# Modulation products of a diffusion backbone run while the last queries of each mixer are rotated, with other rooms for their weights

## The chip, the cores and the metric

The kernel runs on one core of a Trainium2 chip. The metric is the device time of one execution in microseconds, and lower is better. TensorE does the matrix products and the transposes, VectorE (DVE in the rows), ScalarE (ACT) and GpSimd (POOL) the rest; SyncE (SP) issues most of the transfers. A framework lays out each engine's list of instructions before the kernel runs. On the chip every engine works through its own list in that order, and waits where an operand or a room isn't there yet.

## The reference

A backbone of two layers over 512 latent tokens and 256 context tokens, width 1024, in float32:

```python
# layer: SwiGLU (half step) -> token mixing -> SwiGLU (half step)
# each sub-layer:  u = rmsnorm(h, g_pre) * (1 + scale) + shift
#                  h = h + gate * rmsnorm(f(u), g_post)
# shift, scale, gate (9 vectors per layer) = silu(c) @ w_ada + b_ada
def _even_mixer(u, uc, ...):       # layer 0
    xa, ga, q, k, v = _split(u @ w_in, EVEN_SPLITS)
    ...                            # RG-LRU on xa; window attention on q, k, v
    q = _apply_rope(q...); k = _apply_rope(k...)
    o_b = _window_attention(q, k, v, kc, vc, sink_kg)      # 8 heads of 64, 2 kv heads
    y = jnp.concatenate([y_a, o_b], axis=-1) @ w_out
def _odd_mixer(u, uc, ...):        # layer 1
    q = _apply_rope(_rmsnorm(q, q_gain), rope)             # 8 heads of 128, 2 kv heads
    y = _dense_attention(q, k_all, v_all) @ w_out          # 512 queries, 768 keys
```

The modulation is a product of one vector (two: c and the context's) with a matrix of 1024 x 9216 for each layer.

## The kernel before

Tokens are in six tiles of 128 (t = 0 and 1 are the context, 2 to 5 the latents). A float32 product is made as three products of rounded high and low halves.

**Modulation in the background.** Each layer's 9 vectors are computed in blocks p of two vectors. `ada_steps(p)` is a generator: a step k loads two tiles of 128 x 1024 weights (`wa`, halves b = 0 and 1; one transfer of 512 KB each on SP's queue, L126), and does four products of 512 columns with the vector as stationary operand (L129), the four in columns 0-31, 32-63, 64-95 and 96-127 of the array, into one accumulator `ada`. A block has eight steps and a closing part (L136 to L167: bias, transposes, columns, gates). `tick(n)` runs the next n steps where it stands in the code, and the attention calls it three times in each of its groups (a group is a token tile and a kv head). Blocks 3 to 6 run in the even mixer, 7 and 8 in the odd one, and their tiles take rooms `whi` and `wlo`, four each, which the split weights of other phases use. `flush()` at the attention's end runs what is left.

**The mixers.** The q/k/v products of both mixers (`type2`) are done by token tile at their end: the last weights of tile t, then `qkv(t)` or `qf(t)`. There the queries are rotated on VectorE (rope: L1108 to L1111 even, L1393 to L1396 odd), split into halves (`qp`, L1119 and L1120, even), and transposed on TensorE into a PSUM room `ps` (`qT`, L1139, `kT`, L1144; odd `oqT`, L1437). `ps` has two rooms. In the even mixer, the scores of the first two groups (`s`) are made there for t = 4 and 5, and their maximum is one reduction (`sm<-s`, L1171). The attention then makes scores (`s`, L1298 to L1301; odd `os`), transposes the exponentials (`pT`, L1332; odd `opT`) and multiplies them with the values (`av`). Output products follow (`eo0a`; odd `oo0a`).

**Rooms.** `raw` are the three rooms into which weights come before they are split (L179 to L181); `G0` and `G1` hold the gates, one room each, loaded after the attention.

Of the kernel before, what the change touches and what calls it, by code (L numbers as in the profile page):

```python
# [12 lines left out]
F32 = mybir.dt.float32  # L13
# [4 lines left out]
P = 128  # L18
D = 1024
# [9 lines left out]
class Net:  # L29
# [83 lines left out]
    def ada_steps(self, p):  # L113
        nc, cp = self.nc, self.cp
        acc = self.adatile(f"ada{p}")
        for k in range(KD):
            raws = []
            for b in range(2):
                l, j = divmod(2 * p + b, 9)
                src, name = self.a["w_ada"][l, k * P:(k + 1) * P, j * D:(j + 1) * D], f"wa{p}_{k}{b}"  # L120
                if p > 2:

                    t = self.ws.tile([P, D], F32, tag=("whi", "wlo")[b], bufs=4, name=name)
                else:
                    t = self.ws.tile([P, D], F32, tag="bx", bufs=2, name=name)
                nc.sync.dma_start(t, src)  # L126
                raws += [t[:, 0:512], t[:, 512:]]
            for g in range(4):
                ins = nc.tensor.matmul(acc[32 * g:32 * g + 32, :], lhsT=self.sc[:, k, :],  # L129
                                       rhs=raws[g], start=(k == 0), stop=(k == KD - 1), skip_group_check=True)  # L130
                if p == 1:
                    self.late(ins)
            yield
        adt = self.bp.tile([P, 2, 512], F32, tag="bu", bufs=2, name=f"adt{p}")
        rows, post = adt[:, 0], adt[:, 1]
        nc.sync.dma_start(rows, self.a["b_ada"][p])  # L136
        nc.vector.tensor_add(rows, acc, rows)
        kinds = [(2 * p + b) % 9 % 3 for b in range(2)]
        if any(k != 2 for k in kinds):
            tp = self.adatile(f"adt{p}")  # L140
            for q in range(4):
                nc.tensor.transpose(tp[:, q * P:(q + 1) * P], rows[:, q * P:(q + 1) * P], self.ident)
            cols = cp.tile([P, 4, 2, 4], F32, name=f"cols{p}")
            nc.vector.tensor_copy(cols, tp.rearrange("p (q g w) -> p g w q", q=4, g=4)[:, :, 0:2, :])  # L144
            for b in range(2):
                i = 2 * p + b
                l, j = divmod(i, 9)
                if kinds[b] == 0:
                    self.modc[i] = (cols, 2 * b)
                elif kinds[b] == 1:  # L150
                    gs = cp.tile([P, 2, 2, 4], F32, name=f"gs{i}")
                    g = self.gpre[:, l * 3 + j // 3].rearrange("p (g q) -> p g q", g=2)
                    for v in range(2):
                        nc.vector.scalar_tensor_tensor(gs[:, :, v, :], cols[:, 2 * b:2 * b + 2, v, :], 1.0, g,
                                                       op0=ALU.add, op1=ALU.mult)
                    self.gscale[i] = gs
        for b in range(2):
            if kinds[b] != 2:
                continue
            i = 2 * p + b  # L160
            nc.sync.dma_start(post, self.a["post"][p])
            gp = post
            nc.vector.scalar_tensor_tensor(gp, rows, 1.0 if (i % 9) == 5 else 0.5, post, op0=ALU.mult, op1=ALU.mult)
            gd = self.dp.tile([2, D], F32, name=f"gd{i}")
            for h in range(2):
                q = 32 * (2 * b + h)
                nc.sync.dma_start(gd[:, h * 512:(h + 1) * 512], gp[q:q + 2, :])  # L167
            self.growd[i] = gd
# [812 lines left out]
    def even(self, u, gate_i, finish):  # L981
# [132 lines left out]
        def qkv(t, acc):  # L1114
            qk = roped(acc[:, 0:640], t, f"qk{t}")
            q, k = qk[:, 0:512], qk[:, 512:640]
            qp = sb.tile([P, 8, 2, 64], F32R, tag="bu", bufs=2, name=f"qp{t}")
            q3 = q.rearrange("p (h d) -> p h d", h=8)
            nc.scalar.activation(qp[:, :, 0, :], q3, AF.Copy)  # L1119
            nc.vector.tensor_sub(qp[:, :, 1, :], q3, qp[:, :, 0, :].bitcast(F32))  # L1120
            kp = sb.tile([P, 2, 2, 2, 64], F32R, tag="bu", bufs=2, name=f"kp{t}")
            k3 = k.rearrange("p (h d) -> p h d", h=2)
            for e in range(2):
                nc.scalar.activation(kp[:, 0, :, e, :], k3, AF.Copy)
            for e in range(2):
                nc.vector.tensor_sub(kp[:, 1, :, e, :], k3, kp[:, 0, :, e, :].bitcast(F32))
            if t % 3 == 0:
                qst["v"] = self.c3([P, 3, 2, 2, 64], F32R, f"vt{t}")
                qst["q"] = sb.tile([P, 3, 8, P], F32R, tag=("u0h", "u0l")[t // 3], name=f"qt{t}")
            vt = qst["v"][:, t % 3]  # L1130
            v3 = acc[:, 640:768].rearrange("p (h d) -> p h d", h=2)
            nc.scalar.activation(vt[:, :, 0, :], v3, AF.Copy)
            nc.vector.tensor_sub(vt[:, :, 1, :], v3, vt[:, :, 0, :].bitcast(F32))
            vs[t] = vt
            qt = qst["q"][:, t % 3]
            for h in range(2):
                tp = self.ps(f"qT{t}{h}").bitcast(F32R)
                for e in range(4):
                    nc.tensor.transpose(tp[:, e * P:(e + 1) * P], qp[:, 4 * h + e], self.identr)  # L1139
                nc.scalar.activation(qt[:, 4 * h:4 * h + 4, :], tp.bitcast(F32), AF.Copy)  # L1140
            qs[t] = qt
            tp = self.ps(f"kT{t}").bitcast(F32R)
            for e in range(4):
                nc.tensor.transpose(tp[:, e * P:(e + 1) * P], kp[:, e // 2, e % 2], self.identr)  # L1144
            for s in range(2):
                for h in range(2):
                    o = (2 * s + h) * P
                    nc.scalar.activation(kt[s][h][:, t * P:(t + 1) * P], tp[:, o:o + P].bitcast(F32), AF.Copy)
# [221 lines left out]
    def odd(self, u, gate_i, finish):  # L1370
# [17 lines left out]
        def roped(s3, t, nh, w, name):  # L1388
            o = sb.tile([P, nh, P], F32, tag="bx", bufs=2, name=name + "o")
            t2 = sb.tile([P, nh, P], F32, tag="by", bufs=3, name=name + "t")  # L1390
            bc = lambda x: x.unsqueeze(1).to_broadcast([P, nh, x.shape[-1]])
            tb = tab[t - 2][:, w]
            nc.vector.tensor_mul(o, s3, bc(tb[:, 0, :]))  # L1393
            nc.vector.tensor_mul(t2[:, :, 0::2], s3[:, :, 1::2], bc(tb[:, 1, 0::2]))
            nc.vector.tensor_mul(t2[:, :, 1::2], s3[:, :, 0::2], bc(tb[:, 1, 1::2]))
            nc.vector.tensor_add(o, o, t2)  # L1396
            return o
# [22 lines left out]
        def qf(t, acc):  # L1420
            s3 = acc.rearrange("p (h d) -> p h d", h=8)
            o = roped(s3, t, 8, 0, f"oq{t}")
            r = rms(s3, 8, f"oq{t}")
            rn = sb.tile([P, 2, 8], F32, name=f"orq{t}")
            for e in range(2):
                nc.vector.tensor_scalar(rn[:, e, :], r, (sc, -sc)[e], None, op0=ALU.mult)
            rq[t] = rn
            qt = []
            for s in range(2):
                i = 2 * (t - 2) + s  # L1430
                if i % 3 == 0:
                    qtt.append(sb.tile([P, 3, 8, P], F32R, tag=("u0h", "u0l", "u1h")[i // 3], name=f"oqt{i}"))
                qt.append(qtt[i // 3][:, i % 3])
            for h in range(2):
                tp = self.ps(f"oqT{t}{h}")
                for e in range(4):
                    nc.tensor.transpose(tp[:, e * P:(e + 1) * P], o[:, 4 * h + e, :], self.ident)  # L1437
                hs = slice(4 * h, 4 * h + 4)
                t3 = tp.rearrange("p (h n) -> p h n", h=4)
                nc.scalar.activation(qt[0][:, hs, :], t3, AF.Copy)  # L1440
                if t < 3:
                    nc.vector.tensor_sub(qt[1][:, hs, :], t3, qt[0][:, hs, :].bitcast(F32))
                    continue
                if h == 0:
                    whole = self.junk(f"oqr{t}").rearrange("p (h n) -> p h n", h=8)
                raw = whole[:, hs, :]
                nc.scalar.activation(raw, t3, AF.Copy)
                nc.gpsimd.tensor_sub(qt[1][:, hs, :], raw, qt[0][:, hs, :].bitcast(F32))
            qs[t] = qt
# [222 lines left out]
```

## Time and profile before

| | |
|---|---|
| three runs | 2595.28, 2600.66, 2603.51 us (median 2600.66) |
| profiled execution | 2593.1 us; span of its instructions 2591.3 |
| mean granted clock of TensorE | 0.988 |
| TensorE | 2489.6 us busy, 96% |
| VectorE | 1877.6 us, 72% |
| ScalarE | 1290.7 us, 50% |
| GpSimd | 373.3 us, 14% |

The shares are means over the whole span; what a change in a mixer is worth depends on the stretch in which it stands. The even mixer's attention lies at some 720 to 854 us, the odd one's at 2045 to 2160.

### The profile page before, as it was taken

To read this page: it belongs to the slowest core of one execution; us is meant where nothing else is said; L and a number is where in the kernel's file an instruction comes from. 1 tells how busy PE (TensorE), PEld (TensorE's weight loads), DVE (VectorE), ACT (ScalarE), POOL (GpSimd) and SP (SyncE) were. 2 spreads that over 40 slices of the span, in tenths; PEclk is the share of its full clock that TensorE was granted. 3 is DMA by queue.
4 is the path that set the end of the run, shared out by engine and by line. 5 is a ranking of instruction groups with operands and counts; after the bars stand their busy time and mean duration, and the time that the engine had idled before them with its cause. 6 is when DMAs were issued, how large, how long until landed. Compare 5 with 4: busy or idle time off the path is not lost.

```text
span 2591.3 us, 36846 instructions
## 1 busy us (share of the span) xinstructions
PE 2489.6 (96%) x13683; PEld 2188.9 (84%) x13683; DVE 1877.6 (72%) x2946; ACT 1290.7 (50%) x2346; POOL 373.3 (14%) x472
## 2 busy tenths in 40 slices
PE   7999999998999989999999899999998899999998
PEld 5999997878855779999887899998876667899986
DVE  5877777577677687878757787887586666888843
ACT  4433335556665564443456544444465556655532
POOL 4000000122022130000002300001122221300000
PEclk8999999999999999999999999999999999999999
DMA  7677767651387435555776355558764652544552
GB/s 279 215 244 242 242 222 268 227 188 51 111 297 266 166 106 184 199 180 193 270 245 228 136 187 181 194 193 280 238 233 145 209 180 74 191 130 136 158 174 92
DMA packets 187588, 502.37 MB, mean 194 GB/s; under 512 B 17944, under 2 KB 51912, under 8 KB 187408
## 3 DMA queue, kind: packets, MB, share of 16 engines
q1 hardware_dynamic: 157520, 392.27, 44.6%
q0 software_dynamic: 29888, 107.74, 11.7%
q8 instruction: 107, 1.75, 0.3%
q14 instruction: 73, 0.60, 0.1%
HBM read 397.33 MB, written 102.61 MB: 193 GB/s over the span
## 4 chain that ended last, share of the span: by engine, by line
PE 78%; DVE 7%; issue 7%; DMA 3%; ACT 3%; POOL 2%; SPq 0%; POOLq 0%; DVEq 0%; ACTq 0%
PE px L784 18%; PE py L784 12%; PE pz L784 12%; PE dy L729 8%; PE dx L729 5%; PE d11a L935 5%; PE ada L129 3%; PE oq1a L935 1%; PE gu L211 1%; PE gu L212 1%; PE eo0a L935 1%; PE gu L210 1%; PE qkv1a L935 1%; DMA dw<-in_w_down_dram 1%; PE pT L1332 1%
## 5 line engine op out<-in xcount | busy, mean ns | idle before, releaser
L831 ACT ACTIVATE cp<-px 128x384 f32<-128x384 f32 (+1 forms) x160 | 73.2, 457 | 207.3 <-PE px L784 207.2
L837 ACT ACTIVATE h<-cp 128x768 f32<-128x768 f32 (+1 forms) x80 | 63.3, 792 | 195.7 <-DVE cp L861 138.8
L623 POOL DMA_DIRECT2D wt<-wt x33 | 17.7, 537 | 706.6 <-DVE wt L622 681.4
L129 PE MATMUL ada<-wa,sc 128*32 128x512 f32 x512 | 83.4, 610 | 0.5 <-DVE cols L144 0.4
L831 ACT ACTIVATE cp<-pz 128x384 f32<-128x384 f32 (+1 forms) x80 | 37.0, 463 | 87.2 <-PE pz L784 87.0
L861 DVE TENSOR_TENSOR cp<-px,cp 128x768 f32<-128x768 f32 (+1 forms) x80 | 70.8, 884 | 5.1 <-PE px L784 5.0
L839 DVE TENSOR_TENSOR h<-cp,h 128x768 f32<-128x768 f32 (+1 forms) x80 | 71.2, 891 | 2.2
L670 DVE TENSOR_TENSOR dh_2l<-dh,dh_2h 128x768 fp32r<-128x768 f32 x21 | 20.0, 953 | 70.3 <-ACT dh_2h L669 60.8
L220 POOL TENSOR_TENSOR b_2pr<-b_2pv,mhalf 128x1 f32<-128x1 f32 x6 | 9.6, 1602 | 355.7 <-DVE b_2pv L218 355.7
L811 DVE TENSOR_TENSOR w<-w,w 128x512 f32<-128x512 f32 x80 | 55.4, 692 | 2.7
L812 DVE TENSOR_TENSOR w<-w,w 128x512 f32<-128x512 f32 x80 | 55.4, 692 | 2.7
L810 DVE TENSOR_TENSOR w<-w 128x512 f32<-128x512 f32 x80 | 55.2, 691 | 2.4
L809 DVE TENSOR_TENSOR w<-w,w 128x512 f32<-128x512 f32 x80 | 54.6, 682 | 0.0
L613 POOL DMA_DIRECT2D wt<-in_w_down_dram x66 | 35.5, 537 | 113.1 <-DMA wt<-wt 113.1
L1324 POOL TENSOR_SCALAR p<-p,sm 128x256 f32<-128x256 f32 (+2 forms) x48 | 31.9, 677 | 136.3 <-DVE sm L1321 63.1
L846 DVE TENSOR_TENSOR cp<-py,cp 128x384 f32<-128x384 f32 (+1 forms) x80 | 41.4, 518 | 4.8 <-ACT cp L831 3.9
L670 DVE TENSOR_TENSOR dw_0slo<-dw,dw_0shi 128x1024 fp32r<-128x1024 f32 x21 | 25.7, 1225 | 25.6 <-ACT dw_0shi L669 25.3
L831 ACT ACTIVATE cp<-py 128x384 f32<-128x384 f32 (+1 forms) x80 | 36.3, 454 | 14.3 <-PE py L784 13.9
L1223 ACT ACTIVATE optb<-opT 128x512 fp32r<-128x512 f32 x48 | 28.6, 597 | 28.3 <-PE opT L1520 27.9
L1511 POOL TENSOR_SCALAR op<-op,osm 128x768 f32<-128x768 f32 x32 | 30.6, 956 | 75.8 <-DVE osm L1510 53.4
L854 DVE TENSOR_TENSOR cp<-pz,cp 128x384 f32<-128x384 f32 (+1 forms) x80 | 41.4, 518 | 0.0
L1223 ACT ACTIVATE ptb<-pT 128x512 fp32r<-128x512 f32 x44 | 26.3, 597 | 30.3 <-PE pT L1332 29.9
(5878 smaller groups left out, 9634.2 us busy)
## 6 DMA issues: line engine op xcount, KB each, us to landing
w<-in_wgu_dram SPq DMA_DIRECT2D x175, 512.0 KB, 3.5
wa<-in_w_ada_dram SPq DMA_DIRECT2D x138, 512.0 KB, 5.8
dh<-hd SPq DMA_DIRECT2D x105, 384.0 KB, 5.8
wt<-in_w_down_dram POOLq DMA_DIRECT2D x66, 512.0 KB, 4.6
wt<-wt POOLq DMA_DIRECT2D x66, 512.0 KB, 3.4
dw<-wt SPq DMA_DIRECT2D x60, 512.0 KB, 5.4
hd<-h SPq DMA_DIRECT2D x66, 384.0 KB, 2.8
dw<-in_w_down_dram SPq DMA_DIRECT2D x45, 512.0 KB, 7.0
```

The lines of the kernel that those rows point to most:

```text
L129: ins = nc.tensor.matmul(acc[32 * g:32 * g + 32, :], lhsT=self.sc[:, k, :], rhs=raws[g], start=(k == 0), stop=(k == KD - 1), skip_group_ch ...
L729: nc.tensor.matmul(out, lhsT=x[xi][:, js], rhs=w[wi], start=first and p == 0 and xi == wi, stop=p == np_ - 1 and xi == 1, skip_group_check ...
L784: mm = lambda x, y, **kw: nc.tensor.matmul(out, lhsT=x, rhs=y, skip_group_check=True, **kw)
L810: chain(nc.vector.tensor_add(x1, x1, x2))
L811: chain(nc.vector.tensor_add(x2, x3, x2))
L812: chain(nc.vector.tensor_sub(x4, x4, x2))
L831: chain(nc.scalar.activation(t, src, AF.Copy))
L837: chain(nc.scalar.activation(hc, cp[f], AF.Silu))
L839: chain(nc.vector.tensor_mul(hc, cp[f], hc))
L861: chain(nc.vector.tensor_add(cp[1], x.unsqueeze(1).to_broadcast([P, 2, n]), cp[1]))
L935: mm(acc[:, h:min(h + 512, n)], lhsT=x[xi][:, js], rhs=w[h // 512][wi], start=(k == 0 and xi == 0 and wi == 0), stop=(k == nk - 1 and xi = ...
L1223: self.nc.scalar.activation(b[:, n, 0], tp, AF.Copy)
```

## The change

For blocks 3 and 7, the first of each mixer, the tiles of even steps take the three `raw` rooms, and those of odd steps `G0` and `G1`, one room for each half. All eight steps of these blocks run earlier: three right ahead of the query transposes of t = 4, and five ahead of those of t = 5. Their accumulator takes one of the two `ps` rooms there. The other blocks follow in the ticks of the attention, which are as before, so each of them starts eight steps earlier.

```diff
@@ ada_steps
                 src, name = self.a["w_ada"][l, k * P:(k + 1) * P, j * D:(j + 1) * D], f"wa{p}_{k}{b}"
-                if p > 2:
-
+                if p in (3, 7):
+
+                    tag, bufs = (("raw", 3), (f"G{b}", 1))[k % 2]
+                    t = self.ws.tile([P, D], F32, tag=tag, bufs=bufs, name=name)
+                elif p > 2:
                     t = self.ws.tile([P, D], F32, tag=("whi", "wlo")[b], bufs=4, name=name)
@@ qkv in even
             qt = qst["q"][:, t % 3]
+            if t > 3:
+
+                self.tick(3 if t == 4 else 5)
             for h in range(2):
                 tp = self.ps(f"qT{t}{h}").bitcast(F32R)
@@ qf in odd
                 qt.append(qtt[i // 3][:, i % 3])
+            if t > 3:
+
+                self.tick(3 if t == 4 else 5)
             for h in range(2):
                 tp = self.ps(f"oqT{t}{h}")
```

In the rows below, `wa_KB` is the tile of step K and half B of a block, `x2` its two products; the numbers at the ends of names tell buffers apart. The first place is TensorE at the end of the even mixer's q/k/v products. Before:

```order
L935 MATMUL qkv1a_6232<-qkv1w7hi,u_1l 128x256
L1298 MATMUL s_6590<-kth_5903,qt_6080 128x256
L1299 MATMUL s_6590<-ktl_5905,qt_6080 128x256
L1298 MATMUL s_6590<-kth_5903,qt_6080 128x256
L1299 MATMUL s_6590<-ktl_5905,qt_6080 128x256
L1298 MATMUL s_6590<-kth_5903,qt_6080 128x256
L1144 MATMUL kT_6484<-identr,kp_6465 128x128 x4
L1299 MATMUL s_6590<-ktl_5905,qt_6080 128x256
L1298 MATMUL s_6590<-kth_5903,qt_6080 128x256
L1299 MATMUL s_6590<-ktl_5905,qt_6080 128x256
L1139 MATMUL qT_6568<-identr,qp_6558 128x128 x4
L1139 MATMUL qT_6574<-identr,qp_6558 128x128 x4
```

The same place after the change:

```order
L938 MATMUL qkv1a_6232<-qkv1w7hi,u_1l 128x256
L132 MATMUL ada_6472<-wa_30_6593,sc 32x512 x2
L132 MATMUL ada_6472<-wa_31_6595,sc 32x512 x2
L132 MATMUL ada_6472<-wa_40_6601,sc 32x512 x2
L1304 MATMUL s_6655<-kth_5903,qt_6080 128x256
L1305 MATMUL s_6655<-ktl_5905,qt_6080 128x256
...
L132 MATMUL ada_6472<-wa_41_6603,sc 32x512 x2
...
L1145 MATMUL qT_6633<-identr,qp_6583 128x128 x4
L132 MATMUL ada_6472<-wa_50_6609,sc 32x512 x2
L1145 MATMUL qT_6639<-identr,qp_6583 128x128 x4
L132 MATMUL ada_6472<-wa_51_6611,sc 32x512 x2
L132 MATMUL ada_6472<-wa_60_6617,sc 32x512 x2
```

Eight products now stand between the last q/k/v product and the query transposes of t = 5, and the rest of the block among the transposes. On VectorE the reduction of the early scores, which stood ahead of the rotation of t = 5, now stands behind it and just ahead of `qp`.

The second place is TensorE in the middle of the even mixer's attention. Before:

```order
L129 MATMUL ada_6658<-wa_60_6854,sc 32x512 x2
L129 MATMUL ada_6658<-wa_61_6856,sc 32x512 x2
L1298 MATMUL s_6862<-kth_5902,qt_6408 128x512
L1299 MATMUL s_6862<-ktl_5904,qt_6408 128x512
L1301 MATMUL s_6862<-maskr,identr 128x128
```

After:

```order
L132 MATMUL ada_6736<-wa_60_6932,sc 32x512 x2
L1304 MATMUL s_7048<-kth_5903,qt_6408 128x512
L1305 MATMUL s_7048<-ktl_5905,qt_6408 128x512
L1307 MATMUL s_7048<-maskr,identr 128x128
L132 MATMUL ada_6736<-wa_61_6934,sc 32x512 x2
```

The two halves of a step, which stood side by side, have a score between them; this is so in nearly all steps of the mixer after the change.

The third place is TensorE at the end of the odd mixer's query products. Before:

```order
L935 MATMUL oq1a_18391<-oq1w7hi,u_1l 128x512 x2
L210 MATMUL os_18695<-okth_17849,oqt_18374 128x384
L211 MATMUL os_18695<-oktl_17851,oqt_18374 128x384
L212 MATMUL os_18695<-okth_17849,oqt_18374 128x384
...
L1437 MATMUL oqT_18733<-ident,oq5o 128x128 x4
L1437 MATMUL oqT_18742<-ident,oq5o 128x128 x4
```

After:

```order
L215 MATMUL os_18720<-okth_17849,oqt_18374 128x384
L132 MATMUL ada_18638<-wa_30_18758,sc 32x512 x2
L132 MATMUL ada_18638<-wa_31_18760,sc 32x512 x2
L132 MATMUL ada_18638<-wa_40_18766,sc 32x512 x2
L132 MATMUL ada_18638<-wa_41_18768,sc 32x512 x2
L1446 MATMUL oqT_18798<-ident,oq5o 128x128 x4
...
L132 MATMUL ada_18638<-wa_50_18774,sc 32x512 x2
L1446 MATMUL oqT_18807<-ident,oq5o 128x128 x4
```

Eight products stand ahead of the transposes of t = 5, side by side; the block's last steps follow among them.

## Rows read from the trace of the kernel before

**Rows 1.** The page: busy time by engine, and the modulation products' group.

```profile
PE 2489.6 (96%) x13683; PEld 2188.9 (84%) x13683; DVE 1877.6 (72%) x2946; ACT 1290.7 (50%) x2346; POOL 373.3 (14%) x472
...
L129 PE MATMUL ada<-wa,sc 128*32 128x512 f32 x512 | 83.4, 610 | 0.5 <-DVE cols L144 0.4
```

**Rows 2.** Windows, line L129 alone: stretch, us, TensorE busy, weight loads, clock, DMA.

```profile
724.00:853.60 129.60, 44.15 (x256) 6.25 (x256) 0.97 0.79 279
825.50:853.60 28.10, 11.62 (x56) 1.62 (x56) 1.00 0.64 245
```

**Rows 3.** Windows, even mixer: stretch, us; PE, PEld, DVE, ACT, POOL busy; clock, DMA share, GB/s.

```profile
716.00:724.00 8.00, 8.00 (x59) 7.09 (x57) 6.14 (x18) 5.36 (x15) 0.00 (x0) 1.00 0.47 153
724.00:731.00 7.00, 1.50 (x13) 1.22 (x11) 5.79 (x21) 5.44 (x26) 2.40 (x4) 0.85 1.00 392
731.00:736.00 5.00, 5.00 (x27) 2.82 (x25) 2.02 (x6) 3.67 (x14) 1.87 (x4) 0.52 0.62 209
```

**Rows 4.** Timeline of 722 to 736: start, us, instruction, [idle before <- releaser].

```profile
723.03 0.51 PE L935 MATMUL qkv1a<-qkv1w7hi,u_1l 128*128 128x512 f32 x2
...
723.38 0.28 PE L1298 MATMUL s<-kth,qt 128*128 128x256 f32 x1
...
724.11 0.53 PE L1144 MATMUL kT<-identr,kp 128*128 128x128 f32 x4
...
724.78 0.28 PE L1299 MATMUL s<-ktl,qt 128*128 128x256 f32 x1
...
725.10 1.23 DVE L1171 TENSOR_REDUCE sm<-s 128x4 f32<-128x1024 f32 x1 [2.61 <-PE s L1299]
...
726.31 0.82 DVE L1108 TENSOR_TENSOR qk<-qkv1a,rope 128x640 f32<-128x640 f32 x1
...
729.73 0.69 DVE L1120 TENSOR_TENSOR qp<-qk,qp 128x512 fp32r<-128x512 f32 x1
...
730.57 1.23 PE L1139 MATMUL qT<-identr,qp 128*128 128x128 f32 x8 [5.50 <-DVE qp L1120]
```

**Rows 5.** Windows, the rest of the even attention: columns as in Rows 3.

```profile
733.00:825.50 92.50, 91.67 (x581) 53.09 (x580) 66.47 (x179) 54.40 (x138) 22.74 (x34) 0.99 0.83 284
825.50:853.60 28.10, 26.15 (x148) 12.86 (x146) 20.48 (x53) 20.57 (x50) 6.50 (x10) 1.00 0.64 245
```

**Rows 6.** Windows, odd mixer: columns as in Rows 3.

```profile
2046.00:2055.00 9.00, 8.04 (x41) 6.62 (x41) 6.58 (x13) 5.29 (x22) 4.49 (x5) 1.00 0.65 219
2055.00:2061.00 6.00, 0.86 (x6) 0.57 (x5) 5.74 (x7) 3.53 (x14) 3.91 (x5) 0.93 0.96 344
2061.00:2067.00 6.00, 5.86 (x32) 4.58 (x31) 3.10 (x3) 3.03 (x13) 5.39 (x5) 0.79 0.96 361
2067.00:2077.00 10.00, 7.49 (x31) 6.15 (x32) 6.38 (x15) 5.40 (x10) 2.94 (x4) 0.83 0.35 116
2107.00:2117.00 10.00, 10.00 (x61) 6.52 (x59) 6.95 (x15) 5.00 (x10) 2.79 (x3) 1.00 0.58 172
```

**Rows 7.** Timeline of the even attention: runs of modulation products and what follows.

```profile
829.78 1.06 PE L129 MATMUL ada<-wa,sc 128*32 128x512 f32 x8
...
830.78 0.39 PE L1298 MATMUL s<-kth,qt 128*128 128x256 f32 x1
...
841.03 1.05 PE L129 MATMUL ada<-wa,sc 128*32 128x512 f32 x4
842.01 0.66 PE L1332 MATMUL pT<-ident,p 128*128 128x128 f32 x4
```

**Rows 8.** Timeline of the odd mixer, around the queries of t = 5.

```profile
2054.70 1.22 DVE L1393 TENSOR_TENSOR oq5o<-oq1a,tab 128x1024 f32<-128x1024 f32 x1
...
2060.84 1.94 PE L1437 MATMUL oqT<-ident,oq5o 128*128 128x128 f32 x8 [5.14 <-DVE osm L1510]
```

**Rows 9.** Waits of SP's queue (us, times, longest); DMA issues 700 to 860.

```profile
SPq L126 <- PE ada L129: 56.4, 23, 4.2
...
wa<-in_w_ada_dram SPq DMA_DIRECT2D x64, 512.0 KB, 5.4
```

## The prediction

> **What bounds the kernel now.** I read the profile in this order: busy time by engine, then the groups of instructions, then windows over the stretches that the change touches, then the timeline in them. TensorE is busy 2489.6 us of a span of 2591.3, far ahead of VectorE with 1877.6 [rows 1]. So an edit is worth what it does to TensorE: work that it no longer does, idle time that it fills, time at the lower clock that it avoids. The modulation products are 83.4 us of it, 512 records [rows 1]. Each product is recorded twice, so they are 256 products, 64 steps of four; 32 steps lie in the even mixer (44.15 us) [rows 2].
>
> The even mixer has three parts. At the end of the q/k/v products TensorE has 1.50 us of work in the 7 us from 724 to 731 [rows 3]. The timeline shows one gap of 5.50 us, ended by the rotated queries of the last token tile (qp of t=5) [rows 4]. From 731 to 736 the granted clock is 0.52 in the mean, near the lower of the two levels, 1.2 of 2.4 GHz; the engine had stood still just before, and in the stretch ahead of that it had been busy throughout at 1.00 [rows 3]. From 733 to 825.5 TensorE is busy 91.67 of 92.50 us, VectorE 66.47: it is the bound there. The last 28.1 us before the output products hold 26.15 of TensorE, 20.48 of VectorE and 20.57 of ScalarE [rows 5].
>
> The odd mixer looks alike: idle 0.96 of 9 us (2046 to 2055), 5.14 of 6 (2055 to 2061), 2.51 of 10 (2067 to 2077), a clock of 0.79 and 0.83 around the last two, and later stretches with TensorE full and VectorE at 6.95 of 10 [rows 6].
>
> **Products in smaller runs.** The question is what a modulation product costs where it stands. I call products that stand side by side on TensorE, with other work before and behind, a run; each of the four uses 32 of the 128 columns, so they overlap. Four of them start at 829.78 and the next work starts at 830.78: 1.00 us. Two of them start at 841.03 and the next starts at 842.01: 0.98 us [rows 7]. A half run is as dear as a whole one. So I counted runs in the two orders. Before, the even mixer has 41 runs for its 32 steps, the odd one 21. 44.15 us over 41 runs is 1.077 us a run [rows 2]. In the changed order the odd mixer has 21 again, and the even one 59: the tiles of one step are loaded apart, and a score or a transpose now stands between nearly all halves, as the second place of the order shows. The 18 more runs cost 18 x 1.077 = **+19.4** (by 0.98: +17.6).
>
> All four products of a run stop other work at both ends: 1.077 us busy a run against 0.98 to 1.00 from start to start leaves at most 0.1 us for the change of shape [rows 2, 7]. The Trainium skill, page "TensorEngine Tiling (Array Packing)", section "Tiling Modes", says that changing the tiling mode drains TensorE. That speaks against this change, which has 36 more such changes, but gives no figure. By the trace it is at most 3.6 us, which the price of a run contains already.
>
> **The gap in the even mixer.** The last q/k/v product starts at 723.03 for 0.51 us. The rotation of t=5 waits on VectorE behind a reduction of early scores that comes at 725.10 for 1.23 us, and starts at 726.31; qp ends at 730.42 [rows 4]. In the changed order that reduction stands behind the rotation and just ahead of qp. TensorE first does two runs, a whole and a half one (2.1), then four pairs of early scores with one half run between (scores from 723.38 to 725.06 with 0.53 of key transposes: 1.1 [rows 4]; and 1.05). They end near 723.5 + 4.3 = 727.8; then come the reduction, 1.23, and qp, 0.69: the transposes start near 729.8. About 2.1 us of gap are left of 5.5: **-3.4** (bounds 0, if the wait only moves behind the runs, and -5.5). Of the 5 us at 0.52 the lower clock costs 5 x 0.48 = 2.4; with a gap less than half as long I take half of it, **-1.2** (0 to -2.4).
>
> **The tail loses its cover.** The steps were spread over the attention; eight now come earlier, so they run out earlier. At the point where the tail begins, six scores before their end, 11 runs are left before, and one after. The tail's 26.15 us hold 11.62 of modulation products [rows 2, 5], so 14.5 of other work. Without them VectorE with 20.48 and ScalarE with 20.57, linked by transposes and copies, set its length. It can't be under 20.6, and with the waits between the two engines I take 23, so the tail gives back 28.1 - 23 = 5.1 of the 11.62. The sum above moved the work at its full price, so the loss is 11.6 - 5.1 = **+6.5** (from 28.1 - 20.6 = 7.5 given back: +4.1; if only 2 are given back: +9.6).
>
> **The gaps in the odd mixer.** Three steps before the transposes of t=4 fill the 0.96 us. Ahead of those of t=5 stand two whole runs, 2.0 us, while VectorE rotates from 2054.70 for some 6 us until 2060.84 [rows 6, 8]. Together **-3.0** (0 if the rotation is late by as much; -8.6 if all of 0.96, 5.14 and 2.51 go). The lower clock cost 6 x 0.21 + 10 x 0.17 = 3.0 there [rows 6]; half of it, **-1.5** (0 to -3.0). The runs are as many as before, and this mixer has TensorE as its bound to the end, so nothing is lost behind.
>
> **The tiles' rooms.** The block that moves has five rooms (three of the raw weights, two of the gates) where eight were. The gates' rooms take steps 1, 3, 5 and 7 one after the other: three reloads, each behind the product that frees the room, and a landing takes 5.4 us [rows 9], so 3 x 5.4 = 16.2 and three runs lie at least between step 1 and step 7. In the changed order some 17 to 19 us of other work lie there: q/k/v products from 716 on, the rotation, the first scores. So TensorE waits 0 to 3 us: **+1** over both mixers. The first weights come while the rooms are free, in the q/k/v products and in the feed-forward part before, where they cost nothing: the DMA share is 0.47 at 716 to 724 [rows 3]. If they delayed a weight that is waited for, it would show as a gap on TensorE of up to one landing, 5.4.
>
> **The sum.** +19.4 - 3.4 - 1.2 + 6.5 - 3.0 - 1.5 + 1 = +17.8 us. The profiled execution took 2593.1 us, 7.6 under the median of the three runs, 2600.66, so it would be 2610.9; on the median, 2618.5. I say **2618**. The distances of the terms to their bounds, added as independent errors (the root of the sum of their squares), are about 7 downward and 6 upward: this case alone reaches from 2611 to 2624.
>
> **Rivals.**
> - Half runs are cheap (the other side: faster). The place is the same 59 runs; if a second half cost no more than its share of the four, 0.5 us, 59 runs would cost no more than the 32 steps do whole, and the +19.4 goes, and the price of the tail falls to its +4.1. Left are -3.4 - 1.2 + 4.1 - 3.0 - 1.5 + 1 = -4.0: 2597 on the median, and 2590 if the gaps also fill by another 7. It decides below 0.5 us a half run; against it stands 0.98 [rows 7]. Chance 0.09.
> - All gaps and clock come back (no change). -5.5 - 2.4 - 8.6 - 3.0 = -19.5, against +19.4, and +4.1 for the tail and 0 for the rooms: +4, or 2605. For it: the stretches are short and the products fit in them. Against it: TensorE's list holds only 3.1 us of them ahead of the queries of t=5 in either mixer. Chance 0.17.
> - The rooms stall TensorE (slower still). SP waited 23 times for modulation products, 56.4 us, 2.45 each [rows 9]. If each of the three reloads has such a wait besides its landing, TensorE stands still 7.4 us a mixer more: +14.8 - 1, some 2632. For it: five rooms instead of eight. Against it: SP's queue has only these loads there. Chance 0.12.
> - The forecast: 0.62.
>
> **Range and chances.** 0.3% of this time, 7.8 us, is about what a measurement can tell from none. The range takes in the second and the third rival and leaves out the first and the ends of the others: 2601 to 2633. Faster is the first rival, 0.09; same is the second, 0.17; slower is the forecast and the third, 0.74.
>
> **What the profile after would show.** Busy time of the modulation products near 103 us, from 83.4, at 512 records: if it stays under 90, the first rival holds. Ahead of the query transposes of t=5 in the even mixer a gap near 2 us, and a clock near 0.75 behind it; ahead of those in the odd one 3 us. From the sixth score before the last to the output products about 23 us, with TensorE busy under 16. A wait of TensorE for a tile of the weights of more than 3 us would speak for the third rival. The forecast falls if the halves don't cost what I read, or if the gaps hold more of the products than the orders show.

## The result and the profile after

The changed kernel takes 2620.74 us (median of four runs, 2618.45 to 2624.11), the one before 2598.91 (2595.28 to 2603.51). The ratio is 1.0086, 95% interval 1.0072 to 1.0100: **21.8 us slower**. The forecast was 2618, in a range of 2601 to 2633.

The profiled execution took 2624.11 us, 3.4 over its median, while that of before lay 5.8 under its own. So the two traces differ by 31 us, 9 more than the medians. The page, busy time by engine and the modulation products' group (L132 is what L129 was):

```profile
PE 2515.3 (96%) x13683; PEld 2196.9 (84%) x13683; DVE 1876.9 (72%) x2946; ACT 1290.1 (49%) x2346; POOL 372.1 (14%) x472
...
L132 PE MATMUL ada<-wa,sc 128*32 128x512 f32 x512 | 100.2, 604 | 1.5 <-DMA wa<-in_w_ada_dram 1.4
```

TensorE is busy 25.7 us longer than in [rows 1] with as many instructions; 16.8 of that is the modulation products, again 512 records. No other engine has more to do.

**Where the time went.** I took the start of the same product in both traces at the borders of the stages; the column is after less before, in us, so a step from row to row is what a stage lost or won.

| first product of | before, us | after - before |
|---|---|---|
| q/k/v products, even mixer | 662.68 | +2.2 |
| output products, even mixer | 853.89 | +21.5 |
| layer 1, first feed-forward part | 1443.47 | +24.7 |
| K and V products, odd mixer | 1952.56 | +32.2 |
| output products, odd mixer | 2181.06 | +27.2 |
| last feed-forward part, second half of the tokens | 2248.80 | +29.5 |

Even mixer +19.3, odd mixer -5.0, and **+7.5 in the feed-forward part ahead of the odd mixer**, where the change has no product at all. These three make +21.8, the measured difference; that it fits to the tenth is chance. The rest, +2.2, +3.2 and smaller steps, stands in stretches whose work is the same; it is of the size by which the profiled executions stand off their medians.

**Even mixer.** Timeline of TensorE in the changed kernel, with the first block's products among the last transposes:

```profile
720.29 2.77 PE L132 MATMUL ada<-wa,sc 128*32 128x512 f32 x20
722.99 0.54 PE L1145 MATMUL qT<-identr,qp 128*128 128x128 f32 x4
...
729.74 0.51 PE L938 MATMUL qkv1a<-qkv1w7hi,u_1l 128*128 128x512 f32 x2
730.18 1.91 PE L132 MATMUL ada<-wa,sc 128*32 128x512 f32 x12
732.02 0.38 PE L1304 MATMUL s<-kth,qt 128*128 128x256 f32 x1
...
732.80 1.05 PE L132 MATMUL ada<-wa,sc 128*32 128x512 f32 x4
733.79 0.38 PE L1305 MATMUL s<-ktl,qt 128*128 128x256 f32 x1
...
736.32 0.55 PE L1145 MATMUL qT<-identr,qp 128*128 128x128 f32 x4 [1.92 <-DVE qp L1123]
```

The gap ahead of the transposes of t = 5 is 1.92 us instead of 5.50 [rows 4]. Two products alone (x4) start at 732.80, the next work at 733.79: 0.99 us for half a step, as in [rows 7]. Six together (x12) hold TensorE 1.84 us, and ten (x20) 2.70, less than two and three runs of 1.0. The windows, all instructions (columns of [rows 3]) and then line L132 alone (columns of [rows 2]):

```profile
724.00:730.70 6.70, 6.49 (x44) 4.37 (x44) 2.65 (x10) 4.95 (x17) 0.93 (x2) 1.00 1.00 377
730.70:736.30 5.60, 3.71 (x24) 1.38 (x16) 4.29 (x10) 1.31 (x4) 1.50 (x2) 1.00 0.82 288
736.30:741.00 4.70, 4.68 (x30) 1.88 (x30) 1.75 (x12) 3.76 (x16) 1.40 (x3) 1.00 0.50 153
...
851.95:875.35 23.40, 17.26 (x92) 12.31 (x90) 21.86 (x54) 21.01 (x50) 6.53 (x10) 0.93 0.32 101
```

```profile
718.00:875.35 157.35, 61.52 (x256) 8.85 (x256) 0.99 0.64 233
...
852.30:875.35 23.05, 0.00 (x0) 0.00 (x0) 0.93 0.32 103
```

The granted clock stays at 1.00 behind the gap, where it was 0.52. The same 32 steps take 61.52 us instead of 44.15 [rows 2]. The tail, counted from the same score product to the output products, takes 23.4 us instead of 27.4 and has no modulation product left; TensorE is busy 17.3 in it, VectorE 21.9, ScalarE 21.0. The same stretch in the kernel before, all instructions and then line L129 alone:

```profile
826.52:853.89 27.37, 25.42 (x143) 12.95 (x139) 20.02 (x50) 20.54 (x47) 6.50 (x10) 1.00 0.62 236
```

```profile
826.52:853.89 27.37, 10.62 (x52) 1.47 (x48) 1.00 0.62 236
```

So TensorE's idle time in the tail grew from 1.95 to 6.14 us, and its other work there from 14.80 to 17.26, at a mean clock of 0.93. The clock fell near the tail's middle:

```profile
864.00:868.00 4.00, 3.15 (x11) 2.21 (x10) 3.93 (x9) 3.95 (x11) 2.43 (x4) 0.62 0.41 144
```

**Odd mixer.** Windows around the queries of t = 5, and timeline rows with their idle time:

```profile
2085.00:2091.50 6.50, 6.50 (x32) 4.58 (x31) 0.92 (x6) 4.88 (x11) 4.29 (x4) 1.00 0.99 380
2091.50:2097.00 5.50, 3.61 (x26) 1.79 (x25) 4.65 (x7) 1.99 (x11) 1.41 (x3) 1.00 0.76 249
2097.00:2107.00 10.00, 9.34 (x50) 4.57 (x50) 4.50 (x9) 5.39 (x18) 6.58 (x6) 1.00 0.84 295
```

```profile
2084.56 0.52 PE L1446 MATMUL oqT<-ident,oq4o 128*128 128x128 f32 x3 [1.02 <-DVE oq4o L1402]
...
2096.93 0.63 PE L1446 MATMUL oqT<-ident,oq5o 128*128 128x128 f32 x4 [1.89 <-DVE osm L1519]
2098.22 0.44 PE L213 MATMUL os<-okth,oqt 128*128 128x384 f32 x1 [0.66 <-ACT oq5q L1388]
2108.73 1.05 PE L132 MATMUL ada<-wa,sc 128*32 128x512 f32 x4 [1.15 <-DMA wa<-in_w_ada_dram]
```

The gap of 5.14 is 1.89, the 2.51 us of idle time in the 10 us behind it are 0.66, and the clock is 1.00 throughout, against 0.79 and 0.83 in [rows 6]. Elsewhere in this mixer TensorE stands still a little longer than before, 1.15 us of it for a tile. The whole mixer, from the first K and V product to the first output product, before and after:

```profile
1952.56:2181.06 228.50, 211.10 (x1069) 156.79 (x1069) 157.45 (x324) 133.21 (x334) 59.80 (x61) 0.97 0.49 160
```

```profile
1984.76:2208.23 223.47, 208.97 (x1068) 152.98 (x1069) 155.34 (x324) 132.78 (x334) 59.25 (x61) 0.99 0.48 161
```

The 5.0 us are 2.9 of idle time (17.40 to 14.50) and 2.1 of busy time.

**Ahead of the odd mixer.** The waits of SP's queue (us, times, longest) and its issues, then TensorE, in the changed kernel:

```profile
SPq L129 <- DVE b_1s L520: 15.1, 1, 15.1
```

```profile
1909.79 0.36 SPq L692 DMA_DIRECT2D dw<-wt  x1
1925.21 0.35 SPq L129 DMA_DIRECT2D wa<-in_w_ada_dram  x1
1925.66 0.38 SPq L688 DMA_DIRECT2D dh<-hd  x1
...
1950.07 0.80 PE L732 MATMUL dx<-dw_8slo,dh_8h 128*128 128x512 f32 x1 [6.29 <-DVE dw_8slo L673]
```

SP issues a weight of the feed-forward part at 1909.79 and then nothing for 15 us. Next in its list stands the second half of block 7's step 1, whose room is `G1`. That room holds a gate of the feed-forward part that is just being finished, for the context's tokens, and SP is released by VectorE's work on the second of these (b_1s). The activations and weights (`dh`, `dw`) queued behind it go out only after that, seven of them within 4 us. The 6.29 us of TensorE end with the low half of a weight that VectorE makes (`dw_8slo`). Here is what stood before it on the other engines in the changed kernel, and then VectorE in the kernel before:

```profile
1938.61 0.61 POOL L525 DMA_DIRECT2D b_2x<-xd  x1 [3.47 <-DMA xd<-b_0x]
...
1940.64 1.06 ACT L672 ACTIVATE dw_8shi<-dw 128x1024 fp32r<-128x1024 f32 x1
...
1945.77 1.28 DVE L527 SCALAR_TENSOR_TENSOR b_2x<-b_2y,b_2pr,b_2x 128x1024 f32<-128x1024 f32 x1 [8.69 <-DMA b_2x<-xd]
...
1948.80 1.22 DVE L673 TENSOR_TENSOR dw_8slo<-dw,dw_8shi 128x1024 fp32r<-128x1024 f32 x1
```

```profile
1915.50 1.23 DVE L670 TENSOR_TENSOR dw_8slo<-dw,dw_8shi 128x1024 fp32r<-128x1024 f32 x1 [0.65 <-ACT dw_8shi L669]
...
1918.64 1.28 DVE L524 SCALAR_TENSOR_TENSOR b_2x<-b_2y,b_2pr,b_2x 128x1024 f32<-128x1024 f32 x1
```

The weight itself had come: ScalarE had made its high half by 1941.70, 2.1 us before TensorE ran out of work at 1943.78. What held the low half is VectorE's list. In it the residual sum of token tile 2 (`b_2x`) now stands ahead of the weight's low half, and VectorE stood still 8.69 us for that sum's operand, which GpSimd loads. In the kernel before the sum stands behind. So the early load brought two things, SP's wait and another order on VectorE, and no run has one without the other: the changed kernel, e3, e4 and e5 below have both, the other eight traces neither. How much of the gap each of them makes is not shown.

### The profile page after: what moved, and what is told of

Its sections match the earlier page's. It is cut to its first block, busy times and chain, and to the rows that moved or that the text cites. A ratio compares the mean times of both kernels' runs of the same rounds, so it can differ in the third digit from the quotient of the medians.

```text
span 2622.3 us, 36837 instructions
## 1 busy us (share of the span) xinstructions
PE 2515.3 (96%) x13683; PEld 2196.9 (84%) x13683; DVE 1876.9 (72%) x2946; ACT 1290.1 (49%) x2346; POOL 372.1 (14%) x472
## 4 chain that ended last, share of the span: by engine, by line
PE 74%; issue 8%; DVE 8%; DMA 5%; ACT 3%; POOL 2%; SPq 0%; POOLq 0%; DVEq 0%; ACTq 0%
PE px L787 16%; PE py L787 11%; PE pz L787 11%; PE dy L732 8%; PE dx L732 5%; PE d11a L938 4%; PE ada L132 3%; DMA w<-in_wgu_dram 1%; PE gu L214 1%; PE gu L215 1%; PE gu L213 1%; PE eo0a L938 1%; PE qkv1a L938 1%; DMA dw<-in_w_down_dram 1%; PE qkv0a L938 1%
## 5 line engine op out<-in xcount | busy, mean ns | idle before, releaser
L626 POOL DMA_DIRECT2D wt<-wt x33 | 17.8, 538 | 710.9 <-DVE wt L625 685.7
L132 PE MATMUL ada<-wa,sc 128*32 128x512 f32 x512 | 100.2, 604 | 1.5 <-DMA wa<-in_w_ada_dram 1.4
L1316 DVE TENSOR_REDUCE mx<-s 128x1 f32<-128x512 f32 (+2 forms) x40 | 27.5, 687 | 24.9 <-PE s L1307 22.1
L834 ACT ACTIVATE cp<-py 128x384 f32<-128x384 f32 (+1 forms) x80 | 36.2, 453 | 13.6 <-PE py L787 13.2
L1517 ACT ACTIVATE op<-os,onm,orq 128x768 f32<-128x768 f32 x32 | 31.8, 993 | 17.1 <-DVE onm L1515 13.6
```

Source lines behind the costliest of these rows:

```text
L834: chain(nc.scalar.activation(t, src, AF.Copy))
```

## The experiments

All times stand beside runs of the kernel before on the same chip: 2596.97 us for e1 to e4, 2596.17 for e5 to e8, 2596.50 for e9 and e10. The theory is that the loss has three parts: more runs that each cost a whole one, a tail that lost its cover, and the stop ahead of the odd mixer that comes with SP's wait. Its main rival is that the halves cost little and something else was slow.

**e1_odd_tiles_late.** SP's wait is taken away by holding the load in its place in the code:

```diff
-                nc.sync.dma_start(t, src)
+                load = nc.sync.dma_start(t, src)
+                if p == 7 and k < 2:
+                    self.late(load)
```

> The changed kernel, but the first four tiles of block 7 are loaded only after the last weights of the odd query products, so that no load of them stands in SP's queue in the feed-forward part before. My theory: in the changed kernel the second half of step 1 waits in SP's queue 15.1 us for a gate's room, and the weights queued behind it come late, which costs about 7.3 us (6.3 of gap and the lower clock after it). Then this kernel takes 2621 - 7 = 2614 us (2611 to 2617), and the gap ahead of dx in front of the odd mixer is gone. Rival: the gap comes from the traffic in that stretch and not from this wait; then 2621 within 2 and the gap stays.

2615.05 us, ratio 1.0071 (1.0059 to 1.0084), +18.1, where the changed kernel has +21.8. By the times alone the two intervals overlap; the trace decides. From layer 1's first part to the odd mixer it loses 0.6 us against the kernel before instead of 7.5, and TensorE has no gap in the place (windows, columns of [rows 3]):

```profile
1932.00:1942.00 10.00, 10.00 (x49) 8.19 (x48) 7.16 (x12) 7.24 (x14) 5.90 (x7) 1.00 0.97 335
1942.00:1949.00 7.00, 7.00 (x36) 5.72 (x35) 6.90 (x14) 5.81 (x12) 2.58 (x3) 1.00 0.95 321
```

Transfers fill 0.97 and 0.95 of the queues' time there, so dense traffic by itself makes no gap. VectorE's list has its old order again too, so this run takes away the early load with all that it brought, and not SP's wait alone.

**e2_even_only and e3_odd_only.** Each has the change in one mixer alone (`p == 3` or `p == 7`, and the tick of that mixer).

> Only the even mixer's part of the change (rooms of block 3 and the two ticks there); the odd one as before. My theory: the even mixer's part costs +19 us by itself (more and smaller runs, the tail without cover, less what the gap gives), so 2599 + 19 = 2618 us, and the gap ahead of the odd mixer is absent. Rival: the parts are not additive, since the later start shifts what the odd mixer meets: then 2610 or under, or over 2624.

> Only the odd mixer's part (rooms of block 7 and its two ticks). My theory: -5 us in the mixer itself and +7.3 from SP's wait ahead of it: 2599 + 2 = 2601 us. Rival (the gaps of the odd mixer don't fill, the -5 in the trace comes from elsewhere): 2599 + 7 = 2606 or more.

e2 took 2620.20 us, ratio 1.0087 (1.0074 to 1.0100), +23.2; in its trace the even mixer alone loses 19.4, and the stretch ahead of the odd one 0.3. e3 took 2600.41, ratio 1.0016 (1.0007 to 1.0024), +3.4: +7.2 ahead of the odd mixer and -4.6 in it. The parts add up to 26.6, some 4 more than the changed kernel's ratio gives (0.86%, 22.4 us); the three intervals are wide enough for that. The even mixer carries the loss.

**e4_whole_steps.** Only the order of the four products in a step is changed:

```diff
-            for g in range(4):
+            for g in (2, 0, 3, 1) if p > 2 else range(4):
```

> The changed kernel, but each step of blocks 3 to 8 issues its products in the order 3, 1, 4, 2, so that the first one needs the tile that lands last, and the four stand side by side in TensorE's list: 32 runs in the even mixer instead of 59, 18 in the odd one instead of 21. My theory (a half run costs as much as a whole one): 30 runs fewer at about 1.04 us, less some 4 us that VectorE and ScalarE then show in the tail: 2621 - 27 = 2594 us (2588 to 2600), modulation products 70 us busy. Rival (halves are not the cost; the loss is the tail's and the clock's): 2621 within 5.

2598.61 us, ratio 1.0008 (0.9998 to 1.0019): +1.6, some 20 us less than the changed kernel's +21.8, with the same moves, rooms and SP's wait (15.1 us again). The rows of L132, from the page, and in the even mixer:

```profile
L132 PE MATMUL ada<-wa,sc 128*32 128x512 f32 x512 | 71.0, 615 | 1.5 <-DMA wa<-in_w_ada_dram 0.9
```

```profile
716.00:854.00 138.00, 35.27 (x256) 5.23 (x256) 0.98 0.71 266
```

61.52 us have become 35.27 for the same 256 records, and the mixer gains 1.3 us instead of losing 19.3. So the halves are shown as the cause of the even mixer's loss. But 26.2 us less work gave 20.5 us less time: TensorE's idle time from the first product of the second half's q/k/v to the output products grew, from 8.5 us in the changed kernel to 13.2 (windows of the changed kernel, then of e4):

```profile
694.02:875.35 181.33, 172.83 (x955) 100.31 (x953) 120.21 (x306) 106.33 (x279) 32.97 (x50) 0.99 0.61 221
```

```profile
693.38:854.00 160.62, 147.43 (x954) 96.26 (x953) 118.23 (x306) 105.94 (x279) 33.18 (x50) 0.98 0.68 249
```

**e5_rooms_only.** The rooms of the change without its ticks.

> Only the other rooms of the change (three raw rooms and the gates' for blocks 3 and 7), without the ticks at the query transposes. My theory: the load of step 1's second half of block 7 again stands in SP's queue ahead of the weights of the feed-forward part, so +7.5 us ahead of the odd mixer, and 81 runs instead of 78, +3: 2597 + 10 = 2607 us (2604 to 2610). Rival (the wait comes from the earlier products, not from the rooms): 2597 to 2601, and no gap ahead of dx before the odd mixer.

2606.80 us, ratio 1.0049 (1.0035 to 1.0063), +10.6. SP's queue again waits 15.1 us in the same place, TensorE has a gap of 3.65 us there and the stretch loses 5.9; the even mixer loses 3.6, with 44 runs instead of 41. The wait, and VectorE's new order with it, come with the rooms, not with the early products.

**e6_whole_and_late, e7_before_whole, e8_two_ticks.** Whole steps can also be had by holding the products in their place in the code. e6 is the changed kernel with this and e1's late loads and e4's order, e7 the kernel before with order and place, e8 is e6 with fewer ticks in the even mixer:

```diff
-                if p == 1:
+                if p == 1 or p > 2:
                     self.late(ins)
```

```diff
-                if e in (0,2,3):
+                if e in ticks:
...
-        self.attention(groups, 1, 8, 6)
+        self.attention(groups, 1, 8, 6, (0, 2))
```

> The changed kernel with both suspects taken away: block 7's first tiles loaded late (as in e1), the four products of each step in the order 3, 1, 4, 2 and kept where the code has them, so that every step is one run (64 in all, 96 in the changed kernel). My theory: whole runs give 22 us (e4), two more runs saved 2, the late loads 6: 2621 - 30 = 2591 us (2587 to 2594). Rival (the two gains overlap, since both fill the same waits): 2597 or more.

> The kernel before the change, with the products of each step in the order 3, 1, 4, 2 and kept where the code has them: 66 runs instead of 78, nothing moved. My theory (a half run costs a whole one): 12 runs at 1.05 us less on the engine that is the bound: 2597 - 11 = 2586 us (2583 to 2590). Against the run before it tells what moving the block is worth at the same count of runs: by the terms of the prediction -9.1 for gaps and clock, +6.5 for the tail, +1 for the rooms, so that run should lie 0 to 3 us under this one. Rival (the halves cost nothing before, VectorE takes the place): 2597 within 3.

> As e6, but the even mixer's attention calls a step at two places of each group instead of three, so that the 24 steps that are left reach to its end and the tail has its cover again. My theory (the tail's loss of +6.5 is lost cover): 5 us under e6, and the tail's last stretch again has TensorE over 80% busy. Rival (in the attention VectorE and ScalarE set the pace throughout): as e6 within 2.

e6 took 2588.86 us, ratio 0.9971 (0.9962 to 0.9980). e7 2591.42, ratio 0.9982 (0.9973 to 0.9991). e8 2585.16, ratio 0.9958 (0.9945 to 0.9970). Modulation products are 68.8, 71.1 and 68.7 us busy. The move itself, at nearly the same count of runs (e6 against e7), is worth -2.6 (the intervals overlap a little), inside the 0 to -3 that the prediction's terms gave. By the traces that is -5.1 in the odd mixer and +3.6 in the even one, where e8 too (-4.5 against the kernel before) is not under e7 (-5.2). So with whole steps the move earns its time in the odd mixer; whole steps with the odd part of the move alone were not run.

e7 fell short: 12 runs fewer gave 4.8 us, not 11. In its trace the even mixer gains 5.2 us for 7 runs fewer and the odd one 4.5 for 5. These are 9.6, by the traces; why the times show half of it stays open. In all eleven traces the two mixers and the stretch ahead of the odd one sum to 0.1 to 4.7 us less than the times show, in e7 to the most. So a part of it is the one trace of the kernel before, which is short outside these stretches.

e8 lies 3.7 under e6 (the intervals overlap), where I expected 5, and the even mixer itself 3.0 by the traces. Its tail, and that of e6 (windows, columns of [rows 3]; from the end of the sixth score product before the last, with the same scores, transposes and value products left), then line L134 alone in e8's:

```profile
825.52:851.28 25.76, 23.01 (x150) 12.64 (x149) 22.39 (x55) 21.61 (x53) 7.00 (x10) 1.00 0.73 257
```

```profile
830.41:853.83 23.42, 16.05 (x90) 11.30 (x89) 20.47 (x53) 21.11 (x52) 7.69 (x10) 1.00 0.29 94
```

```profile
825.52:851.28 25.76, 7.46 (x56) 1.10 (x56) 1.00 0.73 257
```

Seven steps stand in e8's tail, 7.5 us of products, and it is only 2.3 us longer. TensorE is busy 89% of it, as expected. So the tail does hide products, and taking them out of it loses that; of the 5.1 us the mixer as a whole shows 3.0.

**e9_ticks_only and e10_odd_one_tick.** The ticks without the rooms (`p > 99` in place of `p in (3, 7)`), and e8 with one tick for each group in the odd mixer.

> Only the ticks at the query transposes; the tiles of blocks 3 and 7 stay in the rooms of the split weights. TensorE's list has 109 runs instead of 78, in both mixers. My theory (each run about 1.05 us): 31 runs more cost 32 us, the odd gaps give back some 5, the tail's cover costs 7, and the tiles, which must wait until the q/k/v weights leave the rooms, hold TensorE up by 5 to 15 us: 2596 + 45 = 2641 us (2630 to 2650). Rival (the number of runs doesn't matter, the rooms of the change do the harm): 2605 or under.

> As e8, and the odd mixer's attention calls a step at one place of each group instead of three, for the eight steps left there. My theory: TensorE is the bound to the odd mixer's end, so spreading them finds no idle time: as e8, 2585 us within 2. Rival (the odd mixer's tail has lost its cover too): 3 us or more under e8.

e9: 2625.93 us, ratio 1.0111 (1.0096 to 1.0127), +29.4, under my range. The products are 114.9 us busy, +31.5 as expected, but TensorE waited for their tiles only 1.7 us in all: the stalls of 5 to 15 us didn't come. e10: 2584.79, ratio 0.9958 (0.9946 to 0.9971), as e8, as expected: spreading the steps over the odd mixer finds nothing (in the traces it gains 7.3 us against 9.5).

## Why the prediction was right

The size and the sign came out, by 21.8 against 17.8, and so did the mechanism in the even mixer. That the sum is so near is in part luck, since one step failed and small misses on the other side made up for most of it. The terms, measured in the traces:

- **Products in smaller runs: +19.4, measured +17.4** (61.52 - 44.15). Right, and shown by e4. The price was a little high because one of the 41 runs before stood at the lower clock (1.77 us busy, at 734.29), and because six or ten products side by side cost less than their runs at 1.077. With that run in it, 1.077 less 0.98 was no bound for the change of shape either.
- **Gap in the even mixer: -3.4, measured -3.6** (5.50 to 1.92). The chain through the reduction and qp was the right one.
- **Lower clock in the even mixer: -1.2, by the clock's rows -2.4.** I took half; the granted clock stays at 1.00 there, with 1.92 us of idle time left.
- **The tail: +6.5, measured +6.6** (10.6 us of products gone, 27.4 - 23.4 = 4.0 given back); I had put its length at 23, and it is 23.4. e6 and e8 support that it is lost cover. But 2.5 of the 6.6 are TensorE's other work at a lower clock, which I did not have: I had said busy under 16, and it is 17.3.
- **The odd mixer, gaps -3.0 and clock -1.5, measured -5.0 together**, 2.9 of idle time and 2.1 of busy time. In the three places that I named 5.0 of 8.6 us were filled (to 1.02 + 1.89 + 0.66), more than I took; 2.1 came back elsewhere, 1.15 of them as a wait for a tile.
- **Tiles' rooms in the mixers: +1, measured +1.4**, the idle time ahead of L132 for its tiles (the odd mixer's part is in its 5.0 already, the even one's is 0.2).
- **The step that failed: "The first weights come while the rooms are free, ... where they cost nothing".** That was costed at 0, with "a gap on TensorE of up to one landing, 5.4" as the price if it were wrong. The stretch lost 7.5 us, 6.3 of them one gap. `G1` was not free: the gate of the part before was still being read, SP's queue stood behind that load for 15.1 us, and with the load VectorE's list had another order, in which it waited 8.69 us ahead of the weight that TensorE needed. I had looked at the share of the transfers, and not at who reads the room last, what stands behind the load in the queue, and what else changes its place. e1 takes all of it away, e3, e4 and e5 have it again.

The measured terms add up to +20.7 of the 21.8. Of the 7.5 that I had at nothing, 4.6 are made up for by the others: the runs cost 2.0 less, the clock in the even mixer gave back 1.2 more, and the rest is 1.4. Of the signs that I named, the products' busy time came near (100.2 us for 103) and so did the gap in the even mixer; the odd one's is 1.89 for 3, and the clock behind the gap was 1.00 and not 0.75.

The three rivals fell: halves are not cheap (0.99 us in the new trace, e4), the gaps came back in part and the runs' price didn't shrink with it, and TensorE hardly waits for tiles in the mixers (1.4 us in the new trace). The Trainium skill, page "TensorEngine Tiling (Array Packing)", section "Tiling Modes", says that a change of tiling mode drains TensorE. The times of runs below leave some 0.13 us a run, by my estimate, in which that can stand, and no run here separates it from the rest of this or shows what the work behind a run loses by it.

## What to carry to other kernels

Before moving small products into idle time, count in the new order how many separate stretches they make on the engine: here half a step cost what a whole one does, and the scheduler's cutting took back far more than the filled gaps gave. For each load that gets another room, find the last reader of that room at the place where the load is issued, read what stands behind it in the same queue, and compare the lists of the other engines there. Work that covers a stretch bound by other engines should last to its end: with whole steps, late loads and fewer ticks (e8) the same idea is 0.42% faster than the kernel before, 11 us. Of these, 4.8 come with whole steps alone and nothing moved (e7).

## What the runs showed of the hardware

The time of column-wise products does not follow their number. One in 32 of 128 columns held TensorE 0.98 us (the kernel before):

```profile
832.49 1.05 PE L129 MATMUL ada<-wa,sc 128*32 128x512 f32 x2
833.47 0.50 PE L1338 MATMUL av<-ptb,vt 128*128 128x512 f32 x1
```

Two held it 0.98 to 0.99, four 1.00, six together 1.84, ten 2.70. So up to four in the four strips of columns took the time of one, and each further four, or what was left of them, 0.85 to 0.86 more. That leaves some 0.13 us of a run beyond its products (an estimate, 0.99 - 0.86). What a cut step pays is therefore mostly a second 0.86 for products that would have run beside the first, and, as far as these times show, only a little for the break.

The granted clock did not fall after idle times of 1.92 us (even mixer) and 1.89 us (odd), whereas it had been at 0.52 behind 5.50 us and at 0.79 behind 5.14 us before. In the 4.7 us (even) and 10 us (odd) that follow in the new trace its mean is 1.00. But single idle times do not tell all: in the tail of the even mixer it was 0.62 from 864 to 868, where the longest idle time before was 1.54 us and TensorE had been busy 1.96 of the last 4.
